# The gated heads' half of an out-projection as seven block products

## The chip, the cores and the metric

The kernel runs on one core of a Trainium2 chip. Its engines work side by side and wait for one another on semaphores: TensorE (PE, matmuls into the PSUM banks; PEld is its weight load), VectorE (DVE), ScalarE (ACT), GpSimd (POOL) and SyncE (SP), whose queue here issues nearly all DMAs. An accumulating DMA, which adds what it moves to what lies at the target, is issued from GpSimd's queue. The metric is the device time in microseconds of one execution; lower is better. 980 us is the scale.

## The reference

A layer of a decoder on x (1 x 1024 x 1024, float32). Two groups of heads work in parallel on one normed input and share one out-projection:

```python
h = rms_norm(x, pre_g)
z = einsum('bsd,de->bse', h, w_in)          # 7184 columns
qa, ka, va, ga, qb, kb, vb, gb, gk_low = split_columns(z)
oa = diff_attention(qa, ka, va, lam)         # 8 heads, two softmax maps each
oa = rms_norm(oa, subln_g) * (1 - lam_init) * silu(ga)
ob = gla_chunked(qb, kb, vb, log_a)          # 4 gated linear heads, width 256
ob = rms_norm(ob, gla_g) * silu(gb)
y  = einsum('bse,ed->bsd', concatenate([oa, ob], -1), w_out)   # 2048 x 1024
return x + rms_norm(y, post_g)
```

The second half of the last product, ob (1024 x 1024) times the lower 1024 rows of w_out, is what the change is about: "the gated half".

## The kernel before

Every matmul operand of full precision is split in two parts, hi and lo (a rounded copy and the rest), and a product is three matmuls: hi x hi, lo x hi, hi x lo. ScalarE makes hi (`act.copy`), VectorE makes lo (a subtraction). A matmul takes 128 x 128 against 128 x 512.

The work goes through these stages, in TensorE's order.

Projections with w_in. They are already done with seven block products instead of eight: `blocks` makes sums of the blocks of h (tiles h11, h12, h22, s1 to s4), `make_weights` makes differences of the blocks of w_in in tiles w_raw, and `step(i)` runs product n of column pair p as the list `order` says; `snap` and `done` join the products. One call of `go(1)` runs one step, of 12 wide matmuls, and prepares the weights of the three steps after it. Results go to DRAM tensors (`qk_d`, `v_d`, `g_d`, and for the gated heads gq_d, gv_d, gg_d). The first steps use weights loaded ahead by `load_early` (w_early).

Splitting of w_out. `wo_step`, called once a step, loads one 128 x 512 piece of w_out (wo_raw, one buffer), and some steps later splits it and stores both parts in `wod`; 32 pieces in all.

Gated heads. `gla(g)` is a generator that runs through one head in two halves of 512 positions and yields between pieces; `go` takes one piece after each step, from column pair 12 on. At its end each half holds o (2 x 128 x 512: features x positions), normed and gated; it is split there and stored in `mixe`, by row tile.

Then eight last steps of the projections (LEAD), among which the loads for the first attention head stand: `load_qk` loads q, k and ks, where ks holds the same keys as k with hi and lo swapped between the partition halves. A score is two matmuls in one group, q on k and q on ks. The tiles live in the pool kp under the tags q0, q1, k0, k1, ks0, ks1, which the gated heads use before them. `weights(e)` loads the split pieces of w_out that belong to the gated half into tiles that the blocks of h have left.

Attention. `merge` interleaves three streams by a cost written beside each: `all_scores` (scores, softmax), `all_values` (transposed weights, values, norms) and `out_early` (out-projection work that is ready). In `out_early` the gated half goes first: for each of 8 row tiles st it takes the 8 blocks e and two column halves dh into two PSUM banks Y, 24 matmuls a bank (tile ypart), copies a bank out (yst, ScalarE) and stores it in `yd` by SP. Then the first four attention heads' part follows, 12 matmuls a bank, which GpSimd adds to yd by accumulating DMAs. The last four heads' part and the closing norm stand at the end; `seed` takes the sum back from yd.

What sets the order: TensorE's order is that of the program (`mm` pins it), and so are the last loads and stores where `keep_in_program_order` stands. On all other queues, SP's and GpSimd's included, a planner places each instruction where it expects its operands and buffers to be ready; on the chip each queue is then worked off strictly in that order. A wait at the head of SP's queue holds all DMAs behind it; SP also waits for one of eight lanes to be free before each issue.

## Time and profile before

| | us |
|---|---|
| median of 3 runs (978.49 to 981.59) | 981.04 |
| the profiled execution | 980.34 |
| its span | 978.6 |
| TensorE busy | 956.6 |
| VectorE busy | 736.0 |
| ScalarE busy | 600.9 |
| GpSimd busy | 135.3 |

The profile is of one execution, 0.7 us under the median. 1.7 us of it lie around the span. In rows of a timeline the first number is the start, the second the length; an "idle before" in brackets names what ended the wait. Projections run until 630.8 us of the span, attention with the early out-projection until about 929 us, the closing part to the end. The granted clock of TensorE is 1.00 in nearly all stretches. A matmul's own row shows 0.39 us, but matmuls are pipelined: the interval from one to the next counts.

### The profile page before, as it was taken

How to read it: one execution, taken by the hardware profiler on the slowest of the kernel's cores; microseconds unless marked ns; L12 is line 12 of the kernel's file. 1: busy time of each engine (PE TensorE's matmuls, PEld its weight loads, DVE VectorE, ACT ScalarE, POOL GpSimd, SP SyncE). 2: the span in 40 equal slices, each digit the busy share in tenths (PEclk: the TensorE clock that was granted, in tenths of full speed). 3: DMA queues.
4: the chain of work that ended last, by engine and by line, in shares of the span. 5: the costliest groups of instructions: out<-in, count | busy, mean ns of one | idle time of the engine just before them, and what ended most of it. 6: DMA issues, size and time to landing. Idle time of an engine off the chain costs nothing.

```text
span 978.6 us, 15745 instructions
## 1 busy us (share of the span) xinstructions
PE 956.6 (98%) x5338; PEld 829.7 (85%) x5338; DVE 736.0 (75%) x1452; ACT 600.9 (61%) x1164; POOL 135.3 (14%) x142
## 2 busy tenths in 40 slices
PE   6999999999999999999999999999999999999997
PEld 5998988888889998899888888878888888888785
DVE  6986597798766677586786876487888888898554
ACT  8642365486467445445566765366777687887773
POOL 4300000000000010000100100021322222443322
PEclk9999999999999999999999999999999999999999
DMA  9443456646765858897988866997657669994777
GB/s 353 143 123 93 124 148 202 229 169 233 253 234 168 266 183 276 247 299 230 298 254 255 270 191 217 357 300 250 206 173 234 233 202 351 351 283 107 151 209 146
DMA packets 152593, 220.45 MB, mean 225 GB/s; under 512 B 17104, under 2 KB 83664, under 8 KB 152416
## 3 DMA queue, kind: packets, MB, share of 16 engines
q1 hardware_dynamic: 148480, 212.10, 66.5%
q0 software_dynamic: 4032, 7.34, 4.8%
q8 instruction: 42, 0.69, 0.3%
q14 instruction: 39, 0.32, 0.1%
HBM read 133.93 MB, written 88.60 MB: 227 GB/s over the span
## 4 chain that ended last, share of the span: by engine, by line
PE 87%; DMA 4%; DVE 4%; ACT 2%; issue 1%; SPq 1%; POOL 0%; DVEq 0%; ACTq 0%; POOLq 0%
PE x L117 21%; PE y L117 14%; PE z L117 14%; PE ypart L117 13%; PE sc L117 7%; PE po L117 5%; PE yps L117 4%; PE wtr L120 3%; PE gpo L117 2%; DMA ks<-k_d 1%; PE kv L117 1%; DMA wo_raw<-in_w_out_dram 1%; DMA w_raw<-in_w_in_dram 1%; PE gkl_ps L117 1%; DVE w L316 1%
## 5 line engine op out<-in xcount | busy, mean ns | idle before, releaser
L315 ACT CAST w<-w_raw 128x512 fp32r<-128x512 f32 (+1 forms) x164 | 112.4, 688 | 97.2 <-PE y L117 46.2
L316 DVE TENSOR_TENSOR w<-w_raw,w 128x512 fp32r<-128x512 f32 (+1 forms) x164 | 126.5, 773 | 52.1 <-ACT w L315 45.6
L1048 ACT ACTIVATE p<-p,stt 128x896 f32<-128x896 f32 (+7 forms) x128 | 99.3, 777 | 37.7 <-DVE stt L1038 33.6
L427 ACT COPY s<-x 128x512 f32<-128x512 f32 x84 | 49.1, 585 | 86.9 <-PE x L117 83.9
L1054 POOL TENSOR_SCALAR p<-p,stt,lam 128x1024 f32<-128x1024 f32 (+3 forms) x64 | 56.2, 877 | 226.2 <-DVE stt L1053 223.8
L296 DVE TENSOR_TENSOR w_raw<-w_raw 128x512 f32<-128x512 f32 (+1 forms) x96 | 75.8, 790 | 15.4 <-DMA w_raw<-in_w_in_dram 14.1
L1038 DVE CUSTOM_DVE_ANT_0 p<-sc,maskt 128x512 f32<-128x512 f32 (+3 forms) x128 | 74.3, 585 | 14.9 <-PE sc L117 13.8
L775 POOL TENSOR_SCALAR_AFFINE_SELECT gan<-gan 128x512 f32<-128x512 f32 x8 | 17.6, 2198 | 486.3 <-ACT gan L774 486.3
L117 PE MATMUL ypart<-wo_hi,m_hi 128*128 128x512 f32 x192 | 79.6, 414 | 0.1
L117 PE MATMUL y<-h_hi,w 128*128 128x512 f32 x320 | 79.6, 391 | 0.0
L117 PE MATMUL z<-s_hi,w 128*128 128x512 f32 x320 | 79.6, 391 | 0.0
L117 PE MATMUL x<-s_hi,w 128*128 128x512 f32 x320 | 79.6, 391 | 0.0
L117 PE MATMUL ypart<-wo_hi,m_lo 128*128 128x512 f32 x192 | 75.5, 393 | 0.0
L117 PE MATMUL ypart<-wo_lo,m_hi 128*128 128x512 f32 x192 | 75.4, 393 | 0.0
L117 PE MATMUL sc<-k,q 128*128 128x512 f32 (+1 forms) x192 | 69.0, 363 | 1.2 <-DVE stt L1038 1.2
L117 PEld LDWEIGHTS x<-s_hi,w 128*128 128x128 f32 x320 | 59.7, 188 | 12.2
L117 PEld LDWEIGHTS y<-h_hi,w 128*128 128x128 f32 x320 | 59.6, 188 | 12.2
L117 PEld LDWEIGHTS z<-s_hi,w 128*128 128x128 f32 x320 | 59.5, 188 | 12.0
L117 PE MATMUL sc<-ks,q 128*128 128x512 f32 (+1 forms) x192 | 66.1, 347 | 1.0 <-DMA ks<-k_d 1.0
L1096 ACT CAST wt_hi<-wtr 128x512 fp32r<-128x512 f32 (+1 forms) x80 | 42.8, 535 | 25.3 <-PE wtr L120 24.5
L1097 DVE TENSOR_TENSOR wt_lo<-wtr,wt_hi 128x512 fp32r<-128x512 f32 (+1 forms) x80 | 50.6, 633 | 9.1 <-ACT wt_hi L1096 8.5
L1057 DVE SCALAR_TENSOR_TENSOR p<-p,stt,p 128x1024 f32<-128x1024 f32 (+3 forms) x64 | 52.1, 814 | 4.1 <-POOL p L1054 3.9
(224 smaller groups left out, 2237.3 us busy)
## 6 DMA issues: line engine op xcount, KB each, us to landing
w_raw<-in_w_in_dram SPq DMA_DIRECT2D x56, 512.0 KB, 4.5
wo_raw<-in_w_out_dram SPq DMA_DIRECT2D x32, 256.0 KB, 2.8
wo_d<-wo_hi SPq DMA_DIRECT2D x32, 256.0 KB, 2.9
wo_d<-wo_raw SPq DMA_DIRECT2D x32, 256.0 KB, 3.3
q<-q_d SPq DMA_DIRECT2D x32, 256.0 KB, 4.6
k<-k_d SPq DMA_DIRECT2D x32, 256.0 KB, 5.3
ks<-k_d SPq DMA_DIRECT2D x64, 128.0 KB, 6.5
wo_hi<-wo_d SPq DMA_DIRECT2D x16, 512.0 KB, 6.4
```

Source lines behind the costliest of these rows:

```text
L117: tc.keep_in_program_order(pe.matmul(*a, **k))
L120: tc.keep_in_program_order(pe.transpose(dst, src, ident))
L296: dve.tensor_tensor(dst, a, b, ALU.subtract)
L315: act.copy(w[0], src)
L316: dve.tensor_tensor(w[1], src, fp(w[0]), ALU.subtract)
L427: act.copy(b[k], ps)
L1038: ins = dve.tensor_tensor_reduce(p[:, a:e], sc[:, : e - a], maskt[:, NZ + P - (e - a) :] if last else maskt[:, : e - a], 1.0, 3e38 if i == ...
L1048: act.activation(p[:, :n], p[:, :n], AF.Exp, bias=st[:, m : m + 1], scale=-1.0, accum_out=st[:, 2 + m : 3 + m],)
L1054: pool.tensor_scalar(p1[:, :n], p1[:, :n], st[:, 5:6], lam, ALU.mult, ALU.mult)
L1057: dve.scalar_tensor_tensor(p0[:, :n], p0[:, :n], st[:, 4:5], p1[:, :n], ALU.mult, ALU.subtract)
L1096: act.copy(hi[:, :n], pt[:, :n])
L1097: dve.tensor_tensor(lo[:, :n], pt[:, :n], fp(hi[:, :n]), ALU.subtract)
```

## The change

The gated half becomes a 2 x 2 block product with seven products instead of eight (each block 512 x 512). Call the left blocks (positions x features) and the blocks of w_out by rows and columns; product n takes one left matrix, `mixe[n]`, and one right matrix, `wgd[n]`. Products 1, 2 and 3 take plain blocks of w_out; 4 to 7 take sums. Products 1, 2, 4 take plain left blocks; 3, 5, 6, 7 take sums. Signs are carried by scales, so that every sum is an addition.

- Right side: `weight_sums` copies 16 pieces of w_out in DRAM (SP, ws_d) and adds other pieces to them by 16 accumulating DMAs (GpSimd), some of them on earlier sums. `wo_step` then splits 12 plain pieces, 16 sums, 16 pieces for the attention half and 4 pieces of left block 7: 48 instead of 32, with two more buffers until the gated stage begins.
- Left side: each half of a gated head stores o also in DRAM tensors left3 to left7, plain or accumulating; `add_left` adds one such tensor to another. The split of o itself moves into the next half (`gla_tails`). A new generator `gla_sums`, ten pieces after the last gated head, loads the sums for products 5, 6 and 3, splits them and stores them in `mixe`. Its tiles take the tags k0 and q0, k1 and q1, ks0 and ks1.
- `out_early` runs 28 units of 12 matmuls (list U): products 2 and 4 first, then 1, 6, 7 as a chain in one bank, where the bank is copied out after each and goes on accumulating, then 5 and 3 as a second chain. 28 copies instead of 16; 16 plain and 16 accumulating stores to yd. Column half 1 is held with a minus sign, which later copies (`y_tile`, `seed`) take into account.
- `load_left` loads each unit's left tile (0.5 MB), `gla_weights` each product's right matrix (4 loads of 0.5 MB); products 2, 4, 1, 6 before attention, 7, 5, 3 within it.

```diff
+    def weight_sums():
+        adds = []
+        for k in range(HB):
+            for n, src, more in (
+                (5, w_block(0, 1, k), w_block(0, 0, k)), (7, w_block(1, 1, k), w_block(0, 1, k)),
+                (6, w_block(1, 1, k), wsd[5][k]), (4, w_block(1, 0, k), wsd[6][k]),
+            ):
+                sp.dma_start(wsd[n][k], src)
+                adds.append((n, k, more))
+                if len(adds) > 2:
+                    add_weights(*adds.pop(0))
+                yield
+        for add in adds:
+            add_weights(*add)
+            yield
+
+    def add_weights(n, k, more):
+        pool.dma_start(wsd[n][k], more, accum_op=ALU.add, max_dma_last_dim=2048)
+        summed.add((n, k))
...
+            to = {1: (7, 6), 5: (5,), 2: (3,), 4: ()}[n]
+            for m in to:
+                sp.dma_start(lefts[m][g % 2].rearrange("t p c -> p t c"), o)
+            for m in {5: (7,), 4: (5,)}.get(n, ()):
+                pool.dma_start(
+                    lefts[m][g % 2].rearrange("t p c -> p t c"), o, accum_op=ALU.add
                 )
...
+    def add_left(i, n, more):
+        src, dst = (lefts[m][i].rearrange("t p c -> p t c") for m in (more, n))
+        pool.dma_start(dst, src, accum_op=ALU.add)
+
+    def gla_sums():
+        gla_tails.pop()()
+        where = (("k0", "q0"), ("k1", "q1"), ("ks0", "ks1"))
+        units, open_units = [(n, i) for i in range(2) for n in (5, 6, 3)], []
+        add_left(1, 6, 5)
+        for now in range(10):
+            if now == 2:
+                add_left(1, 3, 6)
+            if open_units and open_units[0][0] <= now - 2:
+                _, n, i, x, hi = open_units.pop(0)
+                sign = -1.0 if n == 6 else 1.0
+                lo = x.bitcast(F32R)
+                split(hi, lo, x, sign)
+                for t in range(2):
+                    for part, src in enumerate((hi, lo)):
+                        store_left(n, 2 * i + t, part, src[:, t])
+            if units and (units[0][1] == 0 or now > 3):
+                n, i = units.pop(0)
+                tags = where[(5, 6, 3).index(n)]
+                x = kp.tile([P, 2, 512], F32, tag=tags[0], name="left")
+                hi = kp.tile([P, 2, 512], F32R, tag=tags[1], name="left_hi")
+                sp.dma_start(x, lefts[n][i].rearrange("t p c -> p t c"))
+                open_units.append((now, n, i, x, hi))
+            yield
...
+    GLA_IN = {2: "h11", 4: "h12", 1: "s1", 6: "h22", 7: "h11", 5: "h12", 3: "s1"}
...
+    U = [(n, i) for i in range(4) for n in (2, 4)]
+    U += [(n, i + k) for i in (0, 2) for n in (1, 6, 7) for k in range(2)]
+    U += [(n, i + k) for i in (0, 2) for n in (5, 3) for k in range(2)]
...
+            if n in (2, 4, 1, 5):
+                b = j % 2
+                held[n, i] = y_bank(n, b, "ypart")
+            ps = held[{6: 1, 7: 1, 3: 5}.get(n, n), i]
+            for k in range(HB):
+                hi, lo = wg[n][k // 2]
+                m = lefts_in[j]
+                for a, (u, v) in enumerate(((0, hi), (1, hi), (0, lo))):
+                    first = n in (2, 4, 1, 5) and k == 0 and a == 0
+                    mm(
+                        ps, m[:, u, k, :], v[:, k % 2], start=first,
+                        stop=(k == HB - 1 and a == 2), skip_group_check=n in (6, 7, 3),
+                    )
+                yield 1.0 if j < 4 else 0.69
...
+            y = y_tile(ps)
+            for st, dh, add in {
+                2: ((i, 0, False),), 4: ((4 + i, 0, False),), 1: ((i, 0, True),),
+                6: ((i, 1, False),), 7: ((4 + i, 0, True), (4 + i, 1, False)),
+                5: ((4 + i, 1, True),), 3: ((i, 1, True),),
+            }[n]:
+                if add:
+                    pool.dma_start(yd[st][dh], y, accum_op=ALU.add)
+                else:
+                    kept = sp.dma_start(yd[st][dh], y)
```

More of the change, by code (lines that the diff above doesn't have):

```diff
@@ L574, in hymba_kernel, with w_block @@
     fill = []
[L577 to L593 removed]
+    def w_block(i, j, k):
+        return w_out[0, D + i * 512 + k * P : D + i * 512 + k * P + P, j * 512 : j * 512 + 512]
@@ new lines, in add_weights @@
+    def add_weights(n, k, more):
+        pool.dma_start(wsd[n][k], more, accum_op=ALU.add, max_dma_last_dim=2048)
+        summed.add((n, k))
+    summed = set()
+    sum_steps = weight_sums()
+    wo_todo = [("block", n, k) for k in range(HB) for n in (2, 1, 3)]
+    wo_todo += [("sum", n, k) for k in range(HB) for n in (4, 6, 7, 5)]
+    wo_todo += [("rows", e, dh) for e in range(D // P) for dh in range(2)]
+    wo_todo += [("left", 7, k) for k in range(HB)]
+    wo_open, wo_free, wo_now = [], {"t4": 0, "gup": 0}, [0]
@@ L603, in go @@
             step(i)
-            if order[i][0] > EARLY and not (wide(order[i][0]) and order[i][0] % 2):
-                wo_step(order[i][1])
+            if order[i][0] > EARLY:
+                wo_step()
             if fill and next(fill[0], 0) == 0:
@@ L885, in hymba_kernel @@
     go(order.index((12, 5)) - made[0])
-    fill.append(chain(*(gla(g) for g in range(GLA_HEADS))))
+    del wo_free["gup"]
+    fill.append(chain(*(gla(g) for g in range(GLA_HEADS)), gla_sums()))
     go(len(order) - made[0] - LEAD)
@@ L1378, in seed @@
         opened[b] = None
-        pin(b not in Y, act.copy(ps, yp))
+        pin(b not in Y, act.activation(ps, yp, AF.Copy, scale=-1.0) if dh else act.copy(ps, yp))
     def last_times(st, dh, part, e):
```

247 lines of the change are left out of this document (157 added, 90 removed).

## The prediction

> **What bounds the kernel now.** I read the page first: engine shares, then the chain that ended last, then what TensorE waited for.
>
> ```profile
> span 978.6 us, 15745 instructions
> PE 956.6 (98%) x5338; PEld 829.7 (85%) x5338; DVE 736.0 (75%) x1452; ACT 600.9 (61%) x1164; POOL 135.3 (14%) x142
> PE 87%; DMA 4%; DVE 4%; ACT 2%; issue 1%; SPq 1%; POOL 0%; DVEq 0%; ACTq 0%; POOLq 0%
> PE sc L117 <- DVE stt L1038: 1.2, 2, 0.9
> PE sc L117 <- DMA ks<-k_d: 1.0, 1, 1.0
> ```
>
> TensorE is busy for 98% of the span and makes up 87% of the chain; it is the bound. So a matmul taken away is worth its issue interval in full, and a new wait of TensorE costs its length in full, because no later idle time gives it back. In the attention part its waits are of this size: 1.2 us for the softmax and 1.0 us for a key tile. The windows view says how full the DMA engines are beside it (columns: stretch, TensorE, weight loads, VectorE, ScalarE, GpSimd busy, clock, DMA share, GB/s):
>
> ```profile
> 20.00:35.00 15.00, 15.00 (x128) 14.91 (x127) 13.79 (x24) 11.62 (x22) 8.17 (x8) 1.00 1.01 337
> 35.00:50.00 15.00, 13.68 (x99) 12.75 (x98) 14.85 (x24) 9.85 (x18) 1.70 (x2) 1.00 0.06 20
> 450.00:500.00 50.00, 50.00 (x280) 43.70 (x280) 38.13 (x62) 27.99 (x50) 4.18 (x1) 1.00 0.90 286
> 556.00:602.00 46.00, 46.00 (x220) 38.68 (x219) 34.20 (x55) 31.84 (x59) 0.00 (x0) 1.00 0.62 192
> 602.00:643.00 41.00, 40.61 (x180) 33.20 (x178) 21.69 (x41) 15.13 (x26) 1.20 (x1) 1.00 0.92 324
> 610.00:620.00 10.00, 10.00 (x46) 8.29 (x45) 2.67 (x4) 2.83 (x5) 0.00 (x0) 1.00 1.02 404
> 660.00:800.00 140.00, 140.00 (x752) 119.19 (x751) 114.87 (x315) 100.98 (x220) 35.58 (x38) 1.00 0.65 212
> 800.00:880.00 80.00, 80.00 (x425) 67.97 (x424) 70.03 (x186) 63.68 (x137) 28.33 (x31) 1.00 1.01 326
> ```
>
> Two full stretches matter: 20 to 35 us, and 602 to 643 us, where projections end and attention begins. From 800 to 880 us the DMA engines are just as full, yet TensorE works 80.00 of 80 us: fullness alone costs nothing while loads are asked for early.
>
> **The saving.** The gated half has 8 row tiles x 2 column halves x 8 blocks x 3 = 384 matmuls; seven products of 4 x 4 x 3 make 336. A group of the chain gives the interval:
>
> ```profile
> 915.49 1.38 PE ypart L117 x6
> ```
>
> 1.38 / 6 = 0.23 us, and 48 x 0.23 = 11.0 us. They lie in the attention part, where nothing else is waited for, so I count all 11.0 us as gain.
>
> **The late key tile.** This decides. The first head's swapped keys (tile ks, buffers ks0 and ks1) are loaded early before the change:
>
> ```profile
> 581.18 1.81 SPq L878 DMA_DIRECT2D ks<-k_d  x3
> 589.14 0.51 SPq L878 DMA_DIRECT2D ks<-k_d  x1
> 630.80 0.39 PE L117 MATMUL ypart<-wo_hi,m_hi 128*128 128x512 f32 x1
> 632.55 0.40 PE L117 MATMUL sc<-k,q 128*128 128x512 f32 x1
> 632.79 0.39 PE L117 MATMUL sc<-ks,q 128*128 128x512 f32 x1
> ```
>
> The eight loads go out from 581 to 589 us (first and last row) and are first used at 632.8 us: over 40 us of slack. After the change the last stage of the sums of left blocks (unit 3 of `gla_sums`) lives in the same two buffers. In the built program SP issues, in this order: the load of that unit's second half, twelve loads of block weights, the first stores of the last query/key pair, the four stores of the unit (product 3), the other six of that pair's key stores, four more weight loads, the last sixteen query/key stores, and only then the eight ks loads, then v. TensorE's order is fixed: after the projections nine ypart matmuls, one score matmul on k, then one on ks0, whose two loads are fifth and sixth of the eight. Everything of TensorE is queued behind it; VectorE's minimum, ScalarE's exponential and all later loads that wait for a release follow it.
>
> When do the loads go out? Before, the stores that now stand ahead of them went out here:
>
> ```profile
> 622.13 4.93 SPq L367 DMA_DIRECT2D k_d<-qk_st  x8
> 629.22 7.10 SPq L367 DMA_DIRECT2D q_d<-qk_st  x8
> 638.99 1.19 SPq L367 DMA_DIRECT2D q_d<-qk_hi  x2
> 640.27 2.71 SPq L367 DMA_DIRECT2D q_d<-c  x2
> 646.12 2.38 SPq L878 DMA_DIRECT2D ks<-k_d  x4
> 632.39 0.69 DVE L363 SCALAR_TENSOR_TENSOR c<-c,qk_hi 128x512 fp32r<-128x512 f32 x1 [0.70 <-ACT qk_hi L362]
> DMA to landing us min/median/max: 3.4/4.5/6.1
> DMA to landing us min/median/max: 3.4/6.3/8.6
> ```
>
> (The two landing rows are of tile ks: its eight loads before 600 us, and all 28 from 575 to 700 us.) SP is behind: VectorE's last value is there at 633.1 us, its store is through SP at 640.27 + 2.71 = 643.0. With SP as late as now, plus four stores at 1.19 / 2 = 0.60 us (2.4) and six ks issues at 2.38 / 4 = 0.60 us (3.6), the sixth is out at 649.0 and lands 6.3 us later, at 655.3. TensorE gets there at 630.80 + 10 x 0.23 = 633.1. The wait is 22 us.
>
> Bounds. Floor: SP has no backlog and the last store waits only for VectorE: four stores, six issues and the faster landing, 2.4 + 3.6 + 4.5, a wait of 10.5 us. Ceiling: more bytes stand ahead. In 556 to 602 us there are added five loads of 0.52 MB, twenty stores of 0.26 MB, three sums in DRAM of 0.52 MB, less 1.0 MB of ks: 8.4 MB; at 337 GB/s the stretch has (337 - 192) x 46 us = 6.7 MB to spare, and 1.7 MB over is 5 us. After 602 us come 0.52 + 4 x 0.26 = 1.6 MB into a full stretch, 5 us: a wait of 32 us. I take 25, nearest to the row of SP's own lateness, with a third of the backlog, since ten microseconds at 404 GB/s show that the engines can do more than 337.
>
> The Trainium skill ("DMA: Bandwidth & Descriptors", Where 436 GB/s comes from) puts the ceiling of a lone core's fabric at 435 GB/s. By that the two stretches would take the added bytes with no backlog and the wait would be 22 us, the total 3 us less; the best ten microseconds here, 404 GB/s, are nearer to it than to 337, the full early stretch is not.
>
> Restart: after the wait the array may be slow at first. The nearest row is the kernel's first block against the same form later:
>
> ```profile
> 13.96 3.94 PE L117 MATMUL x<-w,h_hi 128*128 128x256 f32 x16 [0.60 <-ACT h_hi L521]
> 20.35 2.17 PE L117 MATMUL x<-w,h_hi 128*128 128x256 f32 x16
> ```
>
> 3.94 - 2.17 = 1.8 us; 0 to 1.8, taken as 1.8. Against that, the old waits of 1.2 and 1.0 us, which lie in the first 30 us of attention, go, as loads and softmax catch up: -2.2 (0 at worst).
>
> **The start.** Sixteen copies of weight blocks in DRAM and two more raw loads are put on SP ahead of the second early weight load:
>
> ```profile
> 20.01 4.46 SPq L1274 DMA_DIRECT2D out_dram<-in_x_dram  x6
> 27.32 0.94 SPq L236 DMA_DIRECT2D w_early<-in_w_in_dram  x2
> 36.80 0.68 DVE L316 TENSOR_TENSOR w<-w_early,w 128x512 fp32r<-128x512 f32 x1
> 50.44 0.68 DVE L548 TENSOR_TENSOR s_lo<-h,s_hi 128x512 fp32r<-128x512 f32 x1
> 45.74 2.00 PE L117 MATMUL x<-h_hi,w 128*128 128x512 f32 x8
> ```
>
> 18 x 0.26 = 4.7 MB at 337 GB/s are 14 us, in a stretch that is full until 35 us; the load moves from 27 to about 38 us, and the built order has VectorE make this weight's low half thirty instructions after the second early weight instead of nine. Thirty of 0.6 us from 30.4 us on give 50 us, and the matmul at 45.74, which needs it after its first 0.9 us, waits 4.3 us (0 if the cover of 35 to 50 us, where the DMA share is 0.06, is enough and VectorE gains on what it does earlier; 8 if the sixteen sums on GpSimd's queue, as many bytes again, hold the load up too). GpSimd's memsets for the gates stand behind these sums; they were done at 42 us and are used past 70, so that is hidden.
>
> **The rest.** Pre-attention: 16 more raw tiles to split, six wide sums, fewer tails; ScalarE has 30 and VectorE 19 instructions more in all, at 0.6 to 1.3 us, 61% and 75% busy. The gated stage's own transfers rise by some 8 MB over 290 us, while 0.90 full gave no wait (450 to 500 us). 0 to 8, taken as 1: the cover is the weights being made three steps ahead. GpSimd's adds of o stand before the next causal mask on its queue, and wait for values that are older than it.
>
> Attention: 12 more copies out of PSUM, 16 more accumulating stores.
>
> ```profile
> L1255 ACT COPY yst<-ypart x32: 564/587/589, 651.2 to 924.5; 128x512 f32<-128x512 f32 x32
> L1313 POOL DMA_DIRECT2D y_d<-yst x16: 858/881/1054, 835.9 to 925.4; - x16
> POOL p L1054 <- DMA y_d<-yst: 1.6, 1, 1.6
> ```
>
> 7.0 us of ScalarE and 14.1 of GpSimd, in a stretch with ScalarE 72% and GpSimd 25% busy; behind a store stands the scaling of p, which was held 1.6 us once with no wait of TensorE. Twelve more left loads (6.3 MB), twelve weight loads more (6.3) and 16 sums (4.2) make 16.8 MB against (337 - 212) x 140 = 17.5 to spare: 0, by the row of 800 to 880 us. The banks of a chain are written again after twelve matmuls of the other bank, copied out in 0.59 us: 0.
>
> **Sum.** On the profiled execution, 980.3 us (978.6 and 1.7 around it): - 11.0 + 25 + 1.8 - 2.2 + 4.3 + 1 = 999.2. The median of the runs, 981.0, is 0.7 above it: 1000 us, slower by 1.9%.
>
> **Rivals.**
> - Faster: SP is punctual, since its lateness at 643 us came from weight loads that have landed by then. Wait 10.5 us, start and rest 0: 980.3 - 11.0 + 10.5 - 2.2 + 0.7 = 978. It decides where new waits come to less than 10 us. For it: VectorE's value at 633.1. Against: SP took 20.9 us for the stores from 622 to 643, and four more are added. 0.10.
> - Attention becomes bound by DMA: the spare bytes are used up, and seven changes of head wait for ks as long as its slowest landing is over its median, 7 x (8.6 - 6.3) = 16 us: 1016. For: 16.8 of 17.5 MB. Against: TensorE at 80.00 of 80 us. 0.13.
> - The gain is there, but the start pays double (8 us) and the gated stage its 8: 1011, in its weights' waits. 0.05.
> - The forecast itself: 0.72; its own range, from a wait of 22 with nothing else to one of 32 with start and rest at 8: 990 to 1017.
>
> **Numbers.** 980 to 1018 leaves out most of the first rival and some of the second. A difference within 0.3% of 981 us can't be told from none: faster 0.10, same 0.05, slower 0.85.
>
> **What would show it.** In the changed profile: the first score matmul on ks idle for over 20 us, released by ks<-k_d; ks issues of the first head past 640 us instead of at 581; 48 fewer ypart matmuls; a wait of some 4 us at the first x<-h_hi matmul near 46 us; no wait past 30 us into attention. The prediction is wrong if SP has the ks loads out by 638 us, or if waits spread over heads.

## The result and the profile after

| | median of the runs | lowest to highest |
|---|---|---|
| before, run again beside it | 980.15 us | 978.49 to 981.59 |
| after | 1059.51 us | 1057.74 to 1064.39 |

The ratio is 1.0818, with a 95% interval of 1.0777 to 1.0859: slower by 8.2%, where the prediction said 1.9%. The profiled execution has a span of 1056.0 us against 978.6, 77.4 us more. The head of its page, the engines' shares of the chain that ended last, and what TensorE waited for:

```profile
span 1056.0 us, 16013 instructions
PE 963.9 (91%) x5290; PEld 828.5 (78%) x5290; DVE 749.5 (71%) x1471; ACT 615.5 (58%) x1194; POOL 168.9 (16%) x182
PE 50%; DMA 22%; DVE 10%; issue 7%; ACT 5%; SPq 3%; POOL 1%; DVEq 0%; ACTq 0%; POOLq 0%
PE sc L127 <- DMA ks<-k_d: 22.1, 2, 21.6
PE x L127 <- ACT w L325: 19.0, 1, 19.0
PE x L127 <- ACT s L437: 9.7, 5, 3.1
PE ypart L127 <- issue: 6.8, 1, 6.8
PE gms L127 <- ACT sq_hl L936: 3.9, 1, 3.9
```

TensorE has 48 matmuls less (5290 for 5338), as meant, but its share of the chain falls from 87% to 50%, and that of DMAs rises from 4% to 22%: it is no longer the bound over the whole span. The windows view, with the columns of the prediction, shows the start (first three rows), the gated stage and the transition to attention, in all of which TensorE is not always busy, and two stretches of attention where it nearly is:

```profile
20.00:35.00 15.00, 15.00 (x128) 15.00 (x127) 12.47 (x24) 10.41 (x19) 12.36 (x13) 1.00 1.03 312
35.00:50.00 15.00, 10.45 (x88) 10.13 (x86) 14.15 (x23) 8.31 (x15) 4.77 (x6) 0.92 1.08 285
50.00:65.00 15.00, 0.60 (x2) 0.50 (x3) 1.94 (x5) 1.27 (x3) 0.00 (x0) 0.50 0.99 248
335.00:628.00 293.00, 277.37 (x1694) 246.28 (x1694) 198.33 (x302) 157.31 (x278) 20.98 (x13) 0.98 0.85 262
650.00:700.00 50.00, 34.05 (x130) 26.39 (x129) 22.92 (x34) 15.91 (x27) 0.00 (x0) 0.82 1.02 359
744.00:884.00 140.00, 138.45 (x741) 116.96 (x740) 117.36 (x320) 108.49 (x237) 46.69 (x51) 1.00 1.02 343
884.00:964.00 80.00, 80.00 (x427) 67.90 (x427) 71.01 (x188) 64.68 (x139) 34.82 (x36) 1.00 0.97 283
```

For the gated stage, the row of the kernel before is:

```profile
335.00:628.00 293.00, 292.18 (x1705) 258.53 (x1704) 204.93 (x318) 164.87 (x291) 15.85 (x6) 1.00 0.79 254
```

There the DMA share has only gone from 0.79 to 0.85, and the rate from 254 to 262 GB/s. The early stretch from 35 to 50 us, where the DMA share was 0.06, is now full, and so are the next 15 us, in which TensorE does next to nothing. In the timeline this is the second early weight load, put behind copies (it went out at 27.32 us before), and the matmul that needs it (45.74 us before):

```profile
25.20 9.39 SPq L601 DMA_DIRECT2D ws_d<-in_w_out_dram  x10
34.64 9.37 SPq L1452 DMA_DIRECT2D out_dram<-in_x_dram  x6
45.56 2.45 SPq L246 DMA_DIRECT2D w_early<-in_w_in_dram  x2
64.40 3.77 PE L127 MATMUL x<-h_hi,w 128*128 128x512 f32 x8 [18.96 <-ACT w L325]
DMA to landing us min/median/max: 8.8/13.3/18.1
```

(The last row is the landing of w_early.) And this is the place where projections end and attention begins, from the same view:

```profile
679.00 3.68 PE L127 MATMUL z<-s_hi,w 128*128 128x512 f32 x8 [2.26 <-DVE c L450]
690.44 1.19 PE L127 MATMUL ypart<-wg_hi,m_in 128*128 128x512 f32 x2 [6.84 <-issue]
716.62 0.77 PE L127 MATMUL sc<-ks,q 128*128 128x512 f32 x1 [21.58 <-DMA ks<-k_d]
720.09 0.39 PE L127 MATMUL sc<-k,q 128*128 128x512 f32 x1
680.41 1.54 SPq L1095 DMA_DIRECT2D m_in<-mixe  x2
697.72 7.27 SPq L377 DMA_DIRECT2D q_d<-qk_st  x8
708.94 1.19 SPq L377 DMA_DIRECT2D q_d<-c  x2
710.18 5.07 SPq L1026 DMA_DIRECT2D ks<-k_d  x8
```

The ks loads leave SP at 710.18 us, behind the last query and key stores, and the score matmul waits 21.58 us for them. The wait of 6.84 us before is for the first left block (m_in): it goes out at 680.41 us, behind twelve loads of block weights, and takes 9.9 us to land.

Apart from the gated heads' own matmuls, TensorE's order is the same in all kernels here up to the end of the projections, so one can see at which matmul a kernel is how much behind. The table does that for all runs: how much later than in the kernel before (us, from the timelines of the profiled executions) TensorE reaches the matmul that ran there at 100.0 us, then what is lost on the way to the one at 334.8 us, to the one at 628 us (the end of the projections), to the first ypart matmul, to the first score matmul on ks, and to the end. The names are those of the next sections.

| kernel | start | to 335 | to 628 | to ypart | to ks | attention | sum |
|---|---|---|---|---|---|---|---|
| after | 20.1 | 3.8 | 27.0 | 8.7 | 24.2 | -6.4 | 77.4 |
| e2_before_copies | 18.9 | 0.0 | -0.3 | 0.0 | 0.0 | 2.4 | 21.0 |
| e1_copies_later | -0.1 | 25.1 | 24.8 | 8.7 | 23.8 | -6.7 | 75.6 |
| e5_copies_spread | 0.2 | 6.6 | 23.3 | 8.7 | 24.1 | -5.4 | 57.5 |
| f1_no_left_sums | 19.7 | 4.3 | 6.8 | 0.0 | 0.2 | 9.3 | 40.3 |
| f2_no_weight_sums | 0.0 | 2.0 | 3.5 | 8.7 | 24.9 | -4.7 | 34.4 |
| f3_no_sums | 0.8 | 4.7 | -1.4 | 0.0 | 0.3 | 3.8 | 8.2 |
| g1_no_sums_left_early | 0.4 | 2.2 | -1.4 | 0.0 | 0.3 | 1.7 | 3.2 |
| e4_job_each_fourth_step | 19.9 | 3.3 | 51.7 | 1.1 | 0.4 | 12.9 | 89.3 |
| g3_tiles_not_split | 25.9 | 27.6 | 4.2 | 8.8 | 24.3 | -6.8 | 84.0 |
| h2_fetch_in_step | 17.2 | 1.5 | 35.7 | 8.8 | 23.8 | -5.5 | 81.5 |
| h1_fetch_in_step_not_split | 17.5 | 2.4 | 26.1 | 8.8 | 24.3 | -6.4 | 72.7 |
| e3_gated_chain_earlier | 21.5 | 22.3 | 54.6 | 0.0 | 0.2 | 3.3 | 101.9 |
| g4_spread_ks_by_gpsimd | 0.9 | 7.7 | 22.5 | 8.7 | 12.8 | 2.5 | 55.1 |
| h3_no_sum_split | 18.8 | 0.2 | 26.3 | 6.5 | 22.5 | -6.2 | 68.1 |
| g6_all_mended | 1.2 | 12.2 | 23.2 | 8.8 | 15.8 | 0.3 | 61.5 |

So the loss of the changed kernel has three places: the start, the gated stage, and the transition to attention (8.7 + 24.2). The sections that follow take them one by one. Attention is 4.7 to 6.8 us shorter in the kernels that wait over 20 us for ks, and shorter in no other. Each ratio is to the kernel before, run on the same chip.

### The profile page after: what moved, and what is told of

It reads as the page before. It is cut to its first block, busy times and chain, and to the rows that moved or that the text cites. A ratio compares the mean times of both kernels' runs of the same rounds, so it can differ in the third digit from the quotient of the medians.

```text
span 1056.0 us, 16013 instructions
## 1 busy us (share of the span) xinstructions
PE 963.9 (91%) x5290; PEld 828.5 (78%) x5290; DVE 749.5 (71%) x1471; ACT 615.5 (58%) x1194; POOL 168.9 (16%) x182
## 4 chain that ended last, share of the span: by engine, by line
PE 50%; DMA 22%; DVE 10%; issue 7%; ACT 5%; SPq 3%; POOL 1%; DVEq 0%; ACTq 0%; POOLq 0%
PE x L127 10%; PE ypart L127 9%; PE y L127 6%; PE z L127 6%; PE sc L127 6%; PE yps L127 4%; PE po L127 4%; PE wtr L130 2%; DMA left_d<-go 2%; DMA w_early<-in_w_in_dram 2%; DMA wo_raw<-in_w_out_dram 2%; DMA wg_hi<-wg_d 2%; DMA wo_d<-wo_raw 2%; DVE w L326 1%; DMA mixe<-wo_raw 1%
## 5 line engine op out<-in xcount | busy, mean ns | idle before, releaser
L325 ACT CAST w<-w_raw 128x512 fp32r<-128x512 f32 (+1 forms) x164 | 111.1, 685 | 68.0 <-PE y L127 25.9
L1217 ACT ACTIVATE p<-p,stt 128x896 f32<-128x896 f32 (+7 forms) x128 | 99.3, 776 | 61.5 <-DVE stt L1207 59.6
L1207 DVE CUSTOM_DVE_ANT_0 p<-sc,maskt 128x512 f32<-128x512 f32 (+3 forms) x128 | 74.4, 585 | 48.4 <-PE sc L127 47.8
L127 PE MATMUL x<-s_hi,w 128*128 128x512 f32 x320 | 81.9, 399 | 9.7 <-ACT s L437 9.7
L306 DVE TENSOR_TENSOR w_raw<-w_raw 128x512 f32<-128x512 f32 (+1 forms) x96 | 76.1, 793 | 18.1 <-DMA w_raw<-in_w_in_dram 16.7
L127 PE MATMUL z<-s_hi,w 128*128 128x512 f32 x320 | 81.5, 398 | 2.8 <-DVE c L450 2.8
L873 POOL TENSOR_SCALAR_AFFINE_SELECT gan<-gan 128x512 f32<-128x512 f32 x8 | 14.5, 1808 | 411.2 <-ACT gan L872 411.2
L127 PE MATMUL ypart<-wg_hi,m_in 128*128 128x512 f32 x224 | 73.8, 411 | 6.8 <-issue 6.8
L127 PEld LDWEIGHTS x<-s_hi,w 128*128 128x128 f32 x320 | 60.3, 191 | 24.4 <-ACT s L437 12.2
L640 ACT CAST wo_hi<-wo_raw 128x512 fp32r<-128x512 f32 x44 | 27.2, 619 | 87.6 <-DMA wo_raw<-in_w_out_dram 55.8
L641 DVE TENSOR_TENSOR wo_raw<-wo_raw,wo_hi 128x512 fp32r<-128x512 f32 x44 | 30.4, 691 | 59.6 <-ACT wo_hi L640 59.4
L127 PE MATMUL x<-h_hi,w 128*128 128x512 f32 x160 | 41.6, 404 | 19.0 <-ACT w L325 19.0
L127 PEld LDWEIGHTS sc<-ks,q 128*128 128x128 f32 x192 | 36.7, 191 | 27.8 <-issue 22.3
```

Source lines behind the costliest of these rows:

```text
L127: tc.keep_in_program_order(pe.matmul(*a, **k))
L306: dve.tensor_tensor(dst, a, b, ALU.subtract)
L325: act.copy(w[0], src)
L640: act.copy(hi, src)
L641: dve.tensor_tensor(lo, src, fp(hi), ALU.subtract)
L1207: ins = dve.tensor_tensor_reduce(p[:, a:e], sc[:, : e - a], maskt[:, NZ + P - (e - a) :] if last else maskt[:, : e - a], 1.0, 3e38 if i == ...
```

## The start: copies in DRAM

**e2_before_copies** puts only the copies and sums of weight blocks into the kernel before, and reads them nowhere:

```diff
+    sum_steps = weight_sums()          # 16 copies (SP), 16 accumulating (GpSimd)
...
             step(i)
+            if order[i][0] > EARLY:
+                next(sum_steps, None)
```

> The kernel before, with only the sixteen copies and sixteen accumulating transfers of weight blocks added, into DRAM tiles that nobody reads; the out-projection and all else is as before. Theory (these transfers alone make the start late): the matmul at 45.74 us waits 15 to 20 us and the time goes from 980 to 995 to 1002. Rival (they are hidden and something else in the changed kernel delays the start): 980 to 984.

Measured: 1001.13 us, 1.0188 (1.0162 to 1.0214). The timeline shows the changed kernel's start again, with nothing else of the change in it:

```profile
21.58 11.70 SPq L594 DMA_DIRECT2D ws_d<-in_w_out_dram  x14
33.33 8.82 SPq L1310 DMA_DIRECT2D out_dram<-in_x_dram  x6
43.72 2.65 SPq L239 DMA_DIRECT2D w_early<-in_w_in_dram  x2
62.78 3.78 PE L120 MATMUL x<-h_hi,w 128*128 128x512 f32 x8 [17.31 <-ACT w L318]
```

The wait of 17.31 us is there: these 32 transfers alone make 18.9 of the 20.1 us that the changed kernel loses at the start.

**e1_copies_later** and **e5_copies_spread** leave the changed kernel as it is and say only when SP issues the copies: e1 behind the raw weight load of the step in which they stand in the code, e5 two behind each of eight earlier raw weight loads.

```diff
-                sp.dma_start(wsd[n][k], src)
+                with tc.issue_after(last_raw[0]):              # e1
...
+                with tc.issue_after(raw_ins[6 + next(n_copy) // 2]):   # e5
+                    sp.dma_start(wsd[n][k], src)
```

> The changed kernel, with the sixteen DRAM copies of weight blocks queued on SP behind the raw weight load of their own step, so that they no longer stand ahead of the second early weight load and of the copies of x to the output. Theory (the start is lost to these copies and the sixteen accumulating transfers that follow them): the matmul at 64.40 us is back near 46, and the run is 15 to 20 us shorter than the changed kernel's 1059.5, 1040 to 1045. Rival (the start is lost to the two added raw tiles and VectorE's order): still 18 us or more idle before that matmul, 1055 to 1060. Second rival (the bytes cost the same wherever they stand): the start is whole, but the first gated matmul gets as much later as the start gained, 1055 to 1060.

Measured: 1055.49 us, 1.0757 (1.0714 to 1.0800). Its second rival held: the start is whole (-0.1) and 25.1 us are lost on the way to 335 instead. The copies now go out beside the first fetches of weight blocks, and the DMA share there is 0.88:

```profile
168.66 4.37 SPq L603 DMA_DIRECT2D ws_d<-in_w_out_dram  x7
192.72 3.35 SPq L603 DMA_DIRECT2D ws_d<-in_w_out_dram  x4
190.00:260.00 70.00, 56.03 (x216) 44.75 (x215) 50.54 (x82) 42.65 (x74) 5.73 (x7) 0.88 0.88 280
```

> The changed kernel, with the sixteen DRAM copies of weight blocks queued on SP two behind each of eight raw weight loads, the ones that go out from 78 to 147 us in the changed profile, where the DMA engines' share is 0.31 to 0.46. In the run before, queued as late as 168 to 198 us, they gave the start back and cost as much near 223 to 254 us. Theory (only the place costs): the start is 18 to 20 us earlier and nothing comes back later, 1037 to 1043. Rival (accumulating transfers in DRAM cost TensorE about 20 us wherever they stand): 1052 to 1060.

Measured: 1038.19 us, 1.0588 (1.0558 to 1.0619), 21.3 us under the changed kernel. The matmul of 64.40 us is back at 45.92, and the stretch into which the copies moved keeps TensorE busy for 73.22 of 74 us:

```profile
45.92 2.00 PE L127 MATMUL x<-h_hi,w 128*128 128x512 f32 x8
56.00:130.00 74.00, 73.22 (x530) 67.67 (x530) 52.94 (x79) 27.59 (x41) 10.17 (x13) 1.00 0.80 207
```

So the same 32 transfers cost 19 us at the start, 21 from 168 us on, and at most 3 (6.6 for 3.8 on the way to 335) when they are thinly spread where few other transfers run. Place and spread changed together, so which of the two matters is not separated.

## The sums left out

Three kernels leave out the making of sums and keep the seven products, with as many loads in attention. f1 leaves out the sums of left blocks, with the four raw tiles of product 7, f2 those of weight blocks, f3 both.

```diff
-            for m in to:                      # f1: stores of o for the sums, and
+            for m in ():                      # the accumulating transfers, none
...
-        units, open_units = [(n, i) for i in range(2) for n in (5, 6, 3)], []
+        units, open_units = [], []
...
-    wo_todo += [("sum", n, k) for k in range(HB) for n in (4, 6, 7, 5)]     # f2
...
-        next(sum_steps, None)
```

> Leaves out all that makes sums of left blocks (their stores, accumulating transfers, loads, splits and stores of parts, and the four raw tiles of product 7); the products 3, 5, 6 and 7 load another product's left blocks, as many bytes. Theory (these sums stop VectorE and ScalarE where projections end): from 650 us to the first score matmul on ks the 31 us go, and the waits of the gated stage from 358 us on, put down to the fetched weight blocks, stay: 1024 to 1032. Rival (the sums' transfers also make the gated stage's waits): 1005 to 1020.

Measured: 1018.49 us, 1.0369 (1.0335 to 1.0403).

> Leaves out all that makes sums of weight blocks (sixteen copies, sixteen accumulating transfers, sixteen raw tiles with their splits and stores); the products 4 to 7 load another product's weights, as many bytes. With 32 raw tiles, as many as before the change, few are left for the gated stage. Theory (the one raw buffer and its late blocks make that stage's waits): the start gives 20 us and the gated stage 15 to 25, the transition of 31 stays, 1014 to 1026. Rival (the gated stage's waits come from the left sums): only the start, 1036 to 1042.

Measured: 1015.03 us, 1.0337 (1.0322 to 1.0353).

> Leaves out both kinds of sums as in the two runs above; the seven products with their 336 matmuls, their loads and the chains of partial sums in two banks stay. Theory (the products save what their matmuls take, and all the loss is from making the sums): 980 less 11 us, 967 to 975. Rival (the added loads and stores of attention, or the pinned order where projections end, cost something by themselves): 980 to 1000.

Measured: 988.07 us, 1.0074 (1.0050 to 1.0098).

The table tells what each removes. Without the left sums the transition is as before (0.2 for 32.9), so they make it. But half of that gain is lost a little later, since attention is now 9.3 us longer instead of 6.4 shorter. The largest wait in it is for a left block:

```profile
683.57 1.19 PE L127 MATMUL ypart<-wg_hi,m_in 128*128 128x512 f32 x2 [12.50 <-DMA m_in<-mixe]
```

Without the weight sums the start is as before. The gated stage belongs to both: its 27.0 us fall to 6.8 without the left sums, to 3.5 without the weight sums. The two add up to more than their parts: 6.8 and 3.5 us with one of them, 27.0 with both. f2 came out as its theory said, in place and time. But f1 refutes what that theory went by, that the fetched weight blocks alone make the gated stage's waits: they are all fetched there, and 6.8 us are left. f1's own theory, by which these waits stay, fell with it, and its rival held in time and place. The 3.8 us on the way to 335 need not come from the sums: f3, which makes none, loses 4.7 there.

f3 was expected at 967 to 975, the full saving, and its rival held. Its attention is 3.8 us longer than before, not 11.0 shorter. The largest piece stands in the view of waits and the timeline: a left block that SP loads behind the last query and key stores.

```profile
PE ypart L127 <- DMA m_in<-mixe: 10.2, 1, 10.2
633.37 7.40 SPq L377 DMA_DIRECT2D q_d<-qk_st  x8
646.24 0.54 SPq L1091 DMA_DIRECT2D m_in<-mixe  x1
```

**g1_no_sums_left_early** moves that load ahead of the stores:

```diff
     go(2)
-    load_left()
-    load_left()
+    for _ in range(4):
+        load_left()
     go(3)
```

> Leaves out both kinds of sums (as f3_no_sums, 988.1), and SP issues the third and fourth load of left blocks together with the first two, ahead of the last 24 query and key stores instead of behind them. Theory (in f3_no_sums the third load, out at 646.24 us behind those stores, makes the 10.2 us wait where attention begins, and the saving of 11 us is there): the wait falls below 2 us, 974 to 979, under the kernel before. Rival (the stretch is full of transfers, and the key or value loads are late instead): 984 to 989.

Measured: 986.60 us, 1.0057 (1.0033 to 1.0080): the wait for m_in is gone, and still the rival's time came out. Attention is now 1.7 us longer than before. A new wait stands a little later, and TensorE loses a little all along:

```profile
658.58 1.11 PE L130 MATMUL wtr<-ident,p 128*128 128x128 f32 x4 [5.89 <-DVE p L1222]
634.00:665.00 31.00, 23.99 (x108) 19.83 (x108) 20.57 (x63) 16.12 (x37) 6.24 (x7) 0.89 0.95 304
700.00:800.00 100.00, 97.59 (x520) 81.91 (x518) 83.24 (x221) 76.93 (x165) 34.65 (x37) 1.00 1.04 344
800.00:900.00 100.00, 99.09 (x529) 84.09 (x530) 87.77 (x240) 80.83 (x176) 42.71 (x46) 1.00 0.92 268
```

```profile
632.00:665.00 33.00, 30.76 (x149) 24.86 (x149) 25.31 (x77) 19.04 (x44) 6.62 (x8) 1.00 0.95 311
700.00:800.00 100.00, 100.00 (x541) 85.26 (x540) 83.89 (x228) 73.37 (x161) 26.52 (x28) 1.00 0.62 205
```

The first fence is g1, the second the kernel before. Idle time is (31.00 - 23.99) - (33.00 - 30.76) = 4.8 us more in the first window, 2.4 and 0.9 in the next two (TensorE was busy throughout from 800 to 900 us before), and 24 us of work at a clock of 0.89 are, as an estimate, 2.6 us slower: 10.7 us, most of the 12.7 by which this attention misses the saving (11.0 and 1.7). The largest piece, the wait for p, starts on ScalarE:

```profile
653.92 0.59 ACT L1421 COPY yst<-ypart 128x512 f32<-128x512 f32 x1 [6.85 <-DMA y_d<-yst]
```

A unit's copy out of PSUM needs one of two buffers (yst). The store that frees it goes out on SP at 647.15 us, behind the query and key stores, and lands at 653.82. ScalarE stands 6.85 us, with the exponentials that make p behind it in its order. The kernel before copies its first bank at 651.24 us, when those stores are through; the units of 12 matmuls fill their banks sooner. So this is one more transfer late at the same junction, and it comes with the shorter units. From 700 to 800 us the DMA share is 1.04 for 0.62. In the changed kernel none of this shows: its attention starts after a wait of 21.58 us and is 6.4 us shorter, perhaps because loads and stores catch up in that wait. This run sets a bound for this form and order: even if the sums cost nothing, the seven products are no faster than the eight.

## The gated stage

What makes these waits? One reading: ScalarE and VectorE take their instructions in order, the splits of fetched tiles stand among those that feed TensorE, and a late tile stops both. The groups view speaks for it (the number after the second bar is the idle time before these casts; before, then after):

```profile
L584 ACT CAST wo_hi<-wo_raw 128x512 fp32r<-128x512 f32 x32 | 19.8, 619 | 34.9 <-DMA wo_raw<-in_w_out_dram 27.8 <-DMA v_d<-c 3.5 <-issue 2.3
```

```profile
L640 ACT CAST wo_hi<-wo_raw 128x512 fp32r<-128x512 f32 x44 | 27.2, 619 | 87.6 <-DMA wo_raw<-in_w_out_dram 55.8 <-DMA wo_raw<-ws_d 14.8 <-DMA wo_raw<-left_d 6.2
```

**e4_job_each_fourth_step** fetches less often:

```diff
-                wo_free[tag] = now + len(wo_free)
+                wo_free[tag] = now + 2
```

> The changed kernel, with a raw weight block fetched on every fourth step instead of every third while one raw buffer serves; the same number of blocks and bytes. Theory (a load of 3.8 us, two splits of 0.6 and 0.7 and a store of 4 to 6 make the one buffer's turn longer than three steps, so that ScalarE and VectorE stand in their queues for late blocks): ScalarE's idle time before these casts falls from 88 us to below 45, the stretch from 358 to 683 us gets 10 to 20 us shorter, 1040 to 1050. Rival (the bytes themselves fill the DMA engines, and waits spread over all loads): 1056 to 1063.

Measured: 1065.14 us, 1.0856 (1.0823 to 1.0889), not faster than the changed kernel, where 1040 to 1050 was expected. ScalarE's idle time falls to 72.7 us, not below 45. At 560 us of the changed kernel TensorE is 10 us ahead of it, but the last tiles, the left blocks of product 7, now come so late that projections stop for 31.63 us at their end:

```profile
685.37 1.04 ACT L640 CAST left_hi<-left 128x1024 fp32r<-128x1024 f32 x1 [26.15 <-DMA wo_raw<-left_d]
698.35 3.78 PE L127 MATMUL z<-s_hi,w 128*128 128x512 f32 x8 [31.63 <-DVE c L450]
```

The ks wait is gone in this run, and two stand in its place: this one and, in attention, one of 16.8 us for a left block.

**g3_tiles_not_split** stores each fetched tile twice, without a split:

```diff
-            hi, lo = t_c("wo_hi", F32R), raw.bitcast(F32R)
-            split(hi, lo, raw, -1.0 if (kind, n) == ("block", 2) else 1.0)
+            hi = lo = raw.bitcast(F32R)
```

> The changed kernel with every fetched weight or left tile stored twice as it is, not split: leaves out 48 casts of ScalarE and 48 subtractions of VectorE; all loads, stores, copies and accumulating transfers stay, the sums of gla_sums are still split. Theory (in the gated stage ScalarE and VectorE stand in order behind tiles that land late, and TensorE waits for what is queued behind): with no instruction that waits for these tiles, the stretch from 358 to 683 us gets 18 to 28 us shorter; start and transition stay, 1031 to 1042. Rival (the added bytes delay all loads): the waits stay in other loads, 1052 to 1060.

Measured: 1062.70 us, 1.0827 (1.0796 to 1.0858). The gated stage has 4.2 us left, as the theory said, but the time came back before it: 27.6 us to 335 instead of 3.8. The fetches ran ahead: the last one of a weight block went out at 333.2 us instead of 539.3. And the edit did not do all that was expected of it, for an instruction that waits for a late tile is left: its store, on SP's queue, ahead of all later loads. SP's own waits from 260 to 335 us:

```profile
SPq L666 <- DMA wo_raw<-in_w_out_dram: 24.2, 10, 4.3
```

The first number is us in total. Another 21.1 us SP waits at fetches until a store has freed the buffer. So the run did not separate the two readings; the standing has moved from ScalarE and VectorE to SP.

**h2_fetch_in_step** holds each fetch to its step, and **h1_fetch_in_step_not_split** does this without splits:

```diff
-            sp.dma_start(raw, wo_source(*job))
+            with tc.issue_after(last_raw[0]):
+                sp.dma_start(raw, wo_source(*job))
```

> The changed kernel, with each fetch of a weight or left tile queued on SP behind the last raw weight load of its step, as a control for the next run. Both theories: near the changed kernel, 1052 to 1064; three early fetches less at the start may give 0 to 5 us.

> As h2_fetch_in_step, but every fetched tile is stored twice as it is: leaves out 48 casts and 48 subtractions; the transfers and their steps stay. Theory (ScalarE and VectorE standing in order behind late tiles): the stretch from 358 to 683 us gets 15 to 28 us shorter than in h2_fetch_in_step, nothing is lost before. Rival (the transfers delay all loads): it gets less than 6 us shorter.

Measured: h2 1063.82 us, 1.0839 (1.0822 to 1.0855), in the range expected, though it is no plain control: it loses 8.7 us more in the gated stage than the changed kernel; h1 1052.00 us, 1.0724 (1.0702 to 1.0746). To 628 us h2 loses 35.7 and h1 26.1. So 9.6 us, about a quarter of what h2 loses, go with the splits, by ScalarE and VectorE standing behind late tiles or by their own work; both numbers expected for h1 were wrong, and its 26.1 us are hardly less than the changed kernel's 27.0. The other three quarters are there with no fetched tile split (and h3 below, with no left sum split either, has 26.3), and most of them go when one kind of sum goes. So they come with both kinds of transfers together, or with the order in which these are issued. The mean share of the DMA engines, 0.85 for 0.79, does not explain them. SP standing in order behind late tiles is a candidate, but no run tests it, and the kernel before has waits of that kind too (SP waits 20.6 us at these fetches from 335 to 628 us). The cause of this part stays open. The remaining waits of h1 are of 1 to 5 us each, for the sum copies of the projections, the state of the gated heads, an output tile and weights.

## The transition

**e3_gated_chain_earlier** starts the gated heads sooner and shortens their pauses, so that the left sums end thirteen steps earlier:

```diff
-    go(order.index((12, 5)) - made[0])
+    go(order.index((11, 4)) - made[0])
...
             yield
             yield
-            yield
             ms, ib = take_bank([P, 512], "gms")
```

> The changed kernel, with the gated heads' work begun five steps earlier and with one pause less in each of its eight halves, so that the sums of left blocks end thirteen steps earlier; the same work is done. Theory (the first head's key tiles wait for the buffers of the last sums and then for SP's queue): the idle time of 21.6 us before the first score matmul on ks falls below 8 us, the 6.8 us before the first ypart matmul may stay, and the run takes 1036 to 1046 instead of 1059.5. Rival (DMA engines at a share of 1.02 from 650 to 700 us make any load late): the wait stays above 12 us, 1050 to 1062.

Measured: 1083.75 us, 1.1044 (1.1009 to 1.1078), the slowest of all. The wait for ks is gone (0.2 us to ks in the table), as the theory said, but not the time: one of 10.5 us for a left block follows in attention, and 54.6 us are lost in the gated stage. The largest piece, waits view and timeline:

```profile
PE z L127 <- DVE c L450: 25.0, 1, 25.0
646.98 1.06 ACT L643 ACTIVATE left_hi<-left 128x1024 fp32r<-128x1024 f32 x1 [13.38 <-DMA left<-left_d]
```

ScalarE stands 13.38 us for a left sum whose load has not landed, with casts and copies that TensorE needs behind it in its queue. Asked for earlier, the same loads are late again, and stop the projections instead of attention.

**g4_spread_ks_by_gpsimd** builds on e5 and issues the first head's eight ks loads on GpSimd's queue:

```diff
-                    ins = sp.dma_start(fp(t[64 * i : 64 * i + 64, m]), d[1 - i])
+                    ins = (sp if h else pool).dma_start(fp(t[64 * i : 64 * i + 64, m]), d[1 - i])
```

> e5_copies_spread (1038.2), with the eight loads of the first head's swapped keys issued on GpSimd's queue instead of SP's. Theory (SP's order, sixteen query and key stores ahead of them, makes most of the 21.8 us): the wait for ks falls below 9 us, 1024 to 1031. Rival (the buffers are only free when the stores of the last sums have landed, near 675 us here): over 14 us stay, 1032 to 1038.

Measured: 1034.97 us, 1.0541 (1.0496 to 1.0587), 3.2 us under e5, though the two intervals overlap. The time is the rival's, and the wait fell between the two expectations. The loads in e5 (first row) and in g4, then g4's waits:

```profile
689.62 5.07 SPq L1030 DMA_DIRECT2D ks<-k_d  x8
```

```profile
674.52 4.24 POOL L1030 DMA_DIRECT2D ks<-k_d  x8 [52.51 <-DMA k_d<-qk_st]
685.34 0.76 PE L127 MATMUL sc<-ks,q 128*128 128x512 f32 x1 [10.24 <-DMA ks<-k_d]
PE ypart L127 <- DMA m_in<-mixe: 7.7, 1, 7.7
```

SP's order costs 15 us in the issue and 11.6 in the wait (21.81 to 10.24), about half of it. The other half has two parts. GpSimd's queue has to wait until the stores of the last sums free the buffers (the row names another store; the second of theirs lands at 673.93 us), so that its first load goes out only 0.6 us before TensorE gets there. And the load that TensorE needs, the sixth, is out at 677.7 us and takes until 685.3, 7.6 us, where in e5 it took 2.3. Of the 11.6 us only 3 reach the end: the next load, a left block that still stands behind SP's stores, now makes TensorE wait 7.7 us. The Trainium skill ("DMA: Bandwidth & Descriptors", Issuing engines are not separate DMA queues) says that all transfers run on the same 16 DMA engines whoever issues them, and that issuing from several engines saves only the time to initiate them. The slower landing fits the first; the 15 us saved are more than the 5.07 that SP takes for these eight issues, since they were time spent behind other stores in SP's order.

**h3_no_sum_split** is h1 without the splits of the left sums:

```diff
-                split(hi, lo, x, sign)
+                hi = lo = x.bitcast(F32R)
```

> As h1_fetch_in_step_not_split, and the six left sums are stored twice as they are too: leaves out six casts and six subtractions more, with all transfers in place. Theory (the turn of the buffers, a load, two splits and a store, and the engines behind it, make the late transition): from 650 us to the first score matmul on ks it is 10 us or more shorter than in h1_fetch_in_step_not_split. Rival (the transfers and SP's order make it): within 5 us of it.

Measured: 1046.39 us, 1.0656 (1.0630 to 1.0681). From 628 us to ks it loses 29.0 us against 33.1 in h1, so the rival held: the splits make 4.1 us of the transition, transfers and SP's order the rest.

**g6_all_mended** takes g4 with all first left blocks together (as in g1) and more fetches ahead of the gated stage:

```diff
-                wo_free[tag] = now + len(wo_free)
+                wo_free[tag] = now + 1
```

> g4_spread_ks_by_gpsimd, with the four first loads of left blocks together, and a raw buffer asked for again one step after its split, so that two buffers make 29 instead of 22 tiles by the step where gated heads begin; it computes all of the reference. Theory (fewer late tiles in the gated stage, and no late left block): 8 to 14 us less than g4_spread_ks_by_gpsimd, 1010 to 1022, which is still slower than the kernel before. Rival (VectorE, busy 16 to 19 of 20 us from 200 to 260, becomes late there): no less than g4_spread_ks_by_gpsimd.

Measured: 1041.67 us, 1.0617 (1.0582 to 1.0652), worse than g4. To 335 us it loses 12.2 for 7.7, the ks column is 3 us longer, and only attention is 2.2 us shorter. So g4 has the lowest median of the kernels with all the sums, and it is 5.4% slower than the one before.

## Why the prediction was wrong

Slower was right, and so was its first reason. The size was not: 1000 us, range to 1018, against 1059.5. Term by term:

- **The saving, -11.0.** 48 matmuls are gone, and the changed kernel's attention is 6.4 us shorter. The price at which the prediction took attention's added loads, copies and stores, nothing, held only behind the long ks wait: in g1, where attention starts on time, they give all of the saving back. The row of 800 to 880 us, "fullness alone costs nothing", did not carry as far as 632 to 800 us.
- **The late key tile, +25.** The step was right in place: ks is issued behind the stores, at 710.18 us, and the sixth load ends the wait. That the size is near, 21.58, is in part luck. The prediction had SP done with that load 16 us after TensorE was there, 6.3 us to land, and 3 us of backlog on the engines; measured are 19 us (714.0 against 695.0), 2.6 us, and no backlog. From 691.0 to 715.2 us SP issues 34 DMAs one behind another, so its queue is what makes the load late. And g4 shows that SP's order is only half of the cause: without it 10.24 us stay. The ceiling at 337 GB/s was too low: the engines moved 422 GB/s from 679.0 to 685.8 us, near the 435 GB/s that the prediction weighed against it from the Trainium skill ("DMA: Bandwidth & Descriptors", Where 436 GB/s comes from).
- **Restart, +1.8.** The term was right in size for the wait that it was meant for: the eight matmuls from 716.62 to 720.09 us take 3.47 us, where 8 x 0.23 are 1.84, 1.6 more. But TensorE restarted slowly three times at this place, and waited once more than any step said. The block at 679.00 us took 3.68 where it takes 1.98, 1.7 more. Then came a wait of 6.84 us for the first left block, and ten slow matmuls, 4.6 us for 2.3. With the wait of 21.58 these last three are 32.4 of the transition's 32.9 us, which is 6 above 25 + 1.8; the 1.6 us are counted to attention.
- **The start, +4.3 (0 to 8).** This term failed first. It priced 18 transfers by their bytes into a stretch that runs dry at 35 us, and let the sums count only as its upper end. Measured: 20.1, and e2 shows 18.9 from the copies and sums alone. They, and the copies of x pushed behind them, kept the engines full to 65 us at 248 to 285 GB/s, below the 337 assumed. The load that matters went out at 45.56 us, not 38, and the early weight loads took up to 18.1 us to land, where the slowest had taken 9.8. VectorE's order, by which the term was worked out, did not end the wait: TensorE waited for ScalarE's cast of that weight, and ScalarE stood 16.0 us for the load. (Thirty instructions of 0.6 us from 30.4 us on also end at 48.4, not 50; they do with the 0.68 of the rows shown.)
- **The rest, +1 (0 to 8).** This term failed by most. It set the added traffic of the gated stage, some 8 MB over 290 us, against a row with 0.90 of the DMA engines busy and no wait, and took it as nearly free. Measured: 27.0 us in the gated stage, and 3.8 before it, as large as what f3 loses there without any sums. The added bytes did not fill the engines there on average (share 0.85 for 0.79), so a price by bytes could not show the loss. f1 and f2 show that either half of the added work would have cost 3.5 to 6.8 us, near the term's own upper end; together they cost four times that or more. Why they do is open.
- **The rivals.** Faster fell with the waits. Attention bound by DMA (1016) did not show in the changed kernel, whose longest wait from 725 us on is 1.5 us; in g1 something of it is there, with a DMA share of 1.04 from 700 to 800 us and a late store. "Start double and gated stage 8", at 0.05, had the right places and less than half their size (16 us for 20.1 + 27.0).

The sign that would have shown the forecast wrong, waits spread over heads, did not come; the waits spread over the stage before.

## What to carry to other kernels

Sums made by DMA are not free work of an idle unit: they are reads and writes on the engines that feed everything else, and the same 32 transfers cost 19 us, 21 us or at most 3 us by where and how densely they were put. A stage's spare transfer time does not price added traffic: 27.0 us were lost at a mean DMA share of 0.85, and two kinds of traffic cost far more together than the sum of each alone. So leave out each kind and both, and look for every load that an engine waits for in order; a row with full engines and no wait says only that its own loads were early. Mending one late load at a junction where all loads are late moves the wait to the next one (21.8 became 10.2 and 7.7 in g4; e3, e4 and f1 lose the ks wait and get one of 10.5 to 16.8 us for a left block), so look at the junction's sum.

## What was not expected of the hardware

- A busy DMA engine is not a fast one. At a share of about 1.0 the rate was 422 GB/s (679.0 to 685.8 us, mostly loads of block weights), 359 GB/s (650 to 700 us, loads and stores of tiles) and 248 GB/s (50 to 65 us, behind copies and sums in DRAM).
- TensorE's clock falls with its idle time. From 50 to 65 us the granted clock was 0.50, and the eight matmuls after that wait took 3.77 us for the usual 2.00. It can take little idling: after 2.26 us at 679.00 the block still took 3.68, at a clock of 0.50 until 682.4. But it need not: after 2.95 us at 588.63 a block of the same form took 2.11. So the length of a wait alone does not decide it here. The Trainium skill ("TensorE: Matmul & The Clock Gate", Part 1: The HAM clock gate) has the half rate after an idle window of about 3.4 us. The half clock agrees; the 2.26 us wait is shorter than that window, and had a slow block behind it all the same. Where the clock falls, a wait here costs some 1.7 us beyond its length.
